# A decoder block in float32: seven products in another order, feature groups 4, 6, 6, 6, and a compressed attention branch stacked to 128 rows

## The chip, the cores and the metric

The kernel runs on one core of a Trainium2 chip. The metric is the device time of one execution in microseconds (us); each figure for a kernel is the median of several executions. The five engines of the core are called by the short names of the profile: PE (TensorE: matrix products and transposes), PEld (its weight loads), DVE (VectorE), ACT (ScalarE), POOL (GpSimd) and SP (SyncE, which issues most transfers). Each engine works through a list of its own in a fixed order.

## The reference

One block on a sequence of 512 tokens with 1024 features, batch 1, all in float32:

```python
h = rmsnorm(x, norm_mix_w); z = h @ w_in          # split into u, v | q, k_c, v_c, k_s, v_s, k_w, v_w, gates
a = gmlp_group(u, v, ...)                         # spatial gating inside chunks of 128 tokens
kc, vc = compress(k_c, ...), compress(v_c, ...)   # 31 compressed positions for each of 2 key/value heads
o = g0 * attention(q, kc, vc) + g1 * selected(q, k_s, v_s) + g2 * window(q, k_w, v_w)   # 8 heads of 64
x = x + concat(rmsnorm(a), rmsnorm(o)) @ w_o
h = rmsnorm(x, norm_ffn_w)
x = x + (silu(h @ w_gate) * (h @ w_up)) @ w_down  # 2816 hidden features
return rmsnorm(x, final_norm_w)
```

## The kernel before, in words

**Precision.** A float32 operand is held as two parts, a high one (`..h`, a copy on ACT by `copy_a`) and a low one (`..l`, the rest, made on DVE by `sub`). A product of two such operands is three matmuls (`mm3`): high by high, high by low, low by high. Tokens come in four tiles of 128.

**Attention.** For each token tile i and each key/value head kv (four query heads hang on one), `score` makes the scores `s`, DVE takes a minimum, ACT the exponential, POOL scales with the gate (`scale_p`). Then the tile is worked off in units: `turn` transposes four heads of probabilities on PE (`ptp`), splits them into high and low (`PT`: an ACT copy and a DVE subtraction of 512 columns), and `apply` multiplies them with the values `Vt` into one bank `o`. The last unit of each (i, kv) is the compressed branch: `cmp_probs` leaves probabilities `sc` over 32 positions for each head, `turn` transposes 128x32 pieces, and `apply` makes two matmuls with `VC`, whose inputs have 32 rows. After kv = 1, `out_norm` transposes the tile's result (`pto`) for its norm. The output projection `project` (banks `po`: eight for its part 0, then eight for part 1, each of 12 matmuls) stands in PE's list between these steps where the scheduler finds room.

**Feed-forward.** 22 blocks f of 128 hidden features; `gate_up(f)` makes 48 matmuls into `gu`. After the blocks of one group, `down` multiplies by `w_down` in the way of Strassen and Winograd: halves of the tokens and of the output columns, and instead of eight products seven (M1 to M7), each for two token tiles c = 0, 1 and all pairs of blocks in the group, three matmuls each. Banks A, B and C (two each) hold them; a bank is read by DVE in `accumulate`, which adds 128x512 to the stream `x2` (in the rows: x<-pA and the like), and some products go on in the same bank. Their weights come from the raw `wd_r` through differences on DVE (`diffs`, `t2_of`, `t4_of`), an ACT copy and a DVE subtraction, into `wh`, a ring of eight buffers that the gate and up weights share.

**End.** For each token tile the final norm: two squares over half a row on ACT (`rstd_halves`), the power on POOL, a multiplication by the norm's weights on DVE, a scale on ACT for one half and one DVE instruction for the other, and two transfers out.

**What sets the order.** The tile framework's scheduler writes each engine's list from the code's order, the dependencies and the buffers. PE's list is therefore not the code's order, and a change in one place moves instructions in others.

The lines that the prediction speaks of: `score` L543, `turn` L611, `apply` L626, `project` by the helper lines L114 to L116, `accumulate` L748, the two splitting helpers L79 (ACT) and L76 (DVE), the end L827 to L832.

Of the kernel before, what the change touches and what calls it, by code (L numbers as in the profile page):

```python
# [8 lines left out]
F32 = mybir.dt.float32  # L9
F32R = mybir.dt.float32r  # L10
# [8 lines left out]
P = 128  # L19
# [13 lines left out]
FFN_GROUPS = (6, 6, 6, 4)  # L33
# [8 lines left out]
def hybrid_gmlp_nsa_kernel(  # L42
# [282 lines left out]
    VC = cp.tile([32, NKV, P], F32R, name="VC")  # L325
# [20 lines left out]
    def compress_end(nm):  # L346
# [22 lines left out]
        else:  # L369
# [5 lines left out]
            copy_a(VC[:NCMP, :, 0:HD], vc)  # L375
            sub(VC[:NCMP, :, HD:P], vc, VC[:NCMP, :, 0:HD])
# [196 lines left out]
    def cmp_probs(i):  # L573
# [18 lines left out]
        for kv in range(NKV):  # L592
            PC[i, kv] = s[:, kv * 4:kv * 4 + 4]
# [8 lines left out]
    PTs, outs, oraws, rstd_b = {}, {}, {}, [None] * NT  # L602

    def turn(u):
        gi, j, br = UNITS[u]
        i, kv, b0 = GROUPS[gi]
        rows = P if j is not None else 32
        pt = bank("T", [P, 4, P], f"ptp{u}")
        for hh in range(4):
            src = probs[gi][:, hh, br, j * P:(j + 1) * P] if j is not None else PC[i, kv][:, hh]  # L610
            nc.tensor.transpose(pt[:rows, hh], src, ident)  # L611
        ptf = pt.rearrange("p h c -> p (h c)")[:rows]
        PTs[u] = t4([P, 2, S], F32R, f"PT{u}")
        copy_a(PTs[u][:rows, 0], ptf)
        sub(PTs[u][:rows, 1], ptf, PTs[u][:rows, 0])

    def apply(u):
# [3 lines left out]
        rows, v = (32, VC[:, kv]) if last else (P, Vt[:, b0 + br, j, kv])  # L621
# [129 lines left out]

    def down(gi, pairs):
# [5 lines left out]
        banks = {}  # L758
# [29 lines left out]

        product("M1", 0, "A", True, lambda r: r[:, 0, 0])
        for c in range(2):  # L790
            accumulate(2 + c, 0, banks["A", c])
        product("M5", 3, "C", True, lambda r: r[:, 0, 0], diffs)
        for c in range(2):
            accumulate(c, 1, banks["C", c])
        product("M6", 4, "A", False, lambda r: r[:, 0, 0], t2_of)
        for c in range(2):
            accumulate(2 + c, 1, banks["A", c])
        product("M2", 2, "B", True, lambda r: r[:, 1, 0])
        for c in range(2):
# [23 lines left out]
    for t in (2, 3, 0, 1):  # L823
        y = b8([P, DM], F32, f"y{t}")
        r = rstd_halves(x2[t], y, f"y{t}")
        rows = slice(t * P, (t + 1) * P)
        nc.vector.tensor_tensor(out=y[:, 0:512], in0=x2[t][:, 0:512], in1=onw[:, 0:512], op=OP.mult)  # L827
        nc.scalar.activation(y[:, 0:512], y[:, 0:512], AF.Copy, scale=r)
        nc.scalar.dma_start(out[rows, 0:512], y[:, 0:512])
        nc.vector.scalar_tensor_tensor(out=y[:, 512:], in0=x2[t][:, 512:], scalar=r, in1=onw[:, 512:],  # L830
                                       op0=OP.mult, op1=OP.mult)
        nc.sync.dma_start(out[rows, 512:], y[:, 512:])  # L832
# [31 lines left out]
```

## Time and profile before

| | |
|---|---|
| median of 3 runs | 631.84 us (631.25 to 632.08) |
| the profiled execution | 630.91 us, its span 629.2 us |
| PE busy | 606.5 us, 96% of the span |
| DVE busy | 411.3 us, 65% |
| ACT busy | 298.7 us, 47% |
| attention, first compressed scores to the last `o` matmul | 141.0 to 252.3 us |
| feed-forward on PE | 276.5 to 617.8 us |
| after PE's last matmul | 617.8 to 629.2 us |

The span runs from the first to the last instruction of the profiled execution; 1.7 us of its time lie outside. A busy PE is not PE at its peak: matmuls are pipelined, their durations overlap, and what one costs is read from the distance between the starts of two that follow each other.

### The profile page before, as it was taken

To read this page: it belongs to the slowest core of one execution; us is meant where nothing else is said; L and a number is where in the kernel's file an instruction comes from. 1 tells how busy PE (TensorE), PEld (TensorE's weight loads), DVE (VectorE), ACT (ScalarE), POOL (GpSimd) and SP (SyncE) were. 2 spreads that over 40 slices of the span, in tenths; PEclk is the share of its full clock that TensorE was granted. 3 is DMA by queue.
4 is the path that set the end of the run, shared out by engine and by line. 5 is a ranking of instruction groups with operands and counts; after the bars stand their busy time and mean duration, and the time that the engine had idled before them with its cause. 6 is when DMAs were issued, how large, how long until landed. Compare 5 with 4: busy or idle time off the path is not lost.

```text
span 629.2 us, 7754 instructions
## 1 busy us (share of the span) xinstructions
PE 606.5 (96%) x2847; PEld 489.9 (78%) x2847; DVE 411.3 (65%) x735; ACT 298.7 (47%) x544; POOL 68.1 (11%) x113
## 2 busy tenths in 40 slices
PE   7999899999999989999999999999999999999992
PEld 6778778787777667798887888887888888888871
DVE  4752778557887986746377944387844387844596
ACT  5753367467866784444234423234423235423244
POOL 3100100015434570100000000000000000000001
PEclk8999999999999999999999999999999999999997
DMA  8452535541000200059510383310373310350003
GB/s 316 147 140 63 171 107 167 161 172 64 1 2 0 76 26 1 2 162 300 157 51 0 121 247 95 95 45 1 126 242 100 95 41 1 131 170 0 2 0 133
DMA packets 73637, 61.85 MB, mean 98 GB/s; under 512 B 3696, under 2 KB 64128, under 8 KB 73600
## 3 DMA queue, kind: packets, MB, share of 16 engines
q1 hardware_dynamic: 73024, 60.32, 30.8%
q10 hardware_dynamic: 576, 1.05, 0.4%
q8 instruction: 22, 0.36, 0.2%
q14 instruction: 15, 0.12, 0.1%
HBM read 59.27 MB, written 2.10 MB: 98 GB/s over the span
## 4 chain that ended last, share of the span: by engine, by line
PE 87%; DVE 5%; DMA 2%; ACT 2%; POOL 1%; issue 1%; SPq 0%; POOLq 0%; ACTq 0%; DVEq 0%
PE gu L115 13%; PE gu L116 13%; PE gu L114 13%; PE o L626 4%; PE pA L114 3%; PE ptp L611 3%; PE pA L115 3%; PE pA L116 3%; PE s L543 2%; PE po L115 2%; PE po L116 2%; PE po L114 2%; PE pC L114 2%; PE pC L116 2%; PE pC L115 2%; PE z_v L116 1%
## 5 line engine op out<-in xcount | busy, mean ns | idle before, releaser
L115 PE MATMUL gu<-h2l,wg_h 128*128 128x512 f32 x168 | 65.4, 389 | 0.0
L114 PE MATMUL gu<-h2h,wg_h 128*128 128x512 f32 x168 | 65.4, 389 | 0.0
L116 PE MATMUL gu<-h2h,wu_l 128*128 128x512 f32 x168 | 65.4, 389 | 0.0
L115 PE MATMUL gu<-h2l,wu_h 128*128 128x512 f32 x168 | 65.4, 389 | 0.0
L116 PE MATMUL gu<-h2h,wg_l 128*128 128x512 f32 x168 | 65.4, 389 | 0.0
L114 PE MATMUL gu<-h2h,wu_h 128*128 128x512 f32 x168 | 65.4, 389 | 0.0
L79 ACT ACTIVATE wu_h<-wu_r 128x1024 fp32r<-128x1024 f32 x21 | 22.3, 1061 | 65.0 <-PE gu L115 48.5
L76 DVE TENSOR_TENSOR wg_l<-wg_r,wg_h 128x1024 fp32r<-128x1024 f32 x21 | 25.7, 1224 | 41.2 <-ACT wg_h L79 40.9
L675 DVE TENSOR_TENSOR sg<-gu,sg 128x512 f32<-128x512 f32 x22 | 15.2, 692 | 56.4 <-PE gu L116 56.4
L79 ACT ACTIVATE wg_h<-wg_r 128x1024 fp32r<-128x1024 f32 x21 | 22.3, 1060 | 45.7 <-PE gu L115 40.8
L167 POOL TENSOR_TENSOR rstd_y<-s_y,mhalf 128x1 f32<-128x1 f32 x4 | 3.0, 755 | 349.5 <-DVE s_y L164 347.0
L548 ACT ACTIVATE P<-P,nm 128x128 f32<-128x128 f32 (+3 forms) x64 | 35.5, 558 | 7.6 <-DVE nm L546 7.5
L114 PEld LDWEIGHTS gu<-h2h,wu_h 128*128 128x128 f32 x168 | 31.6, 188 | 6.6
L82 POOL TENSOR_SCALAR P<-P,sm 128x128 f32<-128x128 f32 (+3 forms) x64 | 33.6, 544 | 28.3 <-DVE sm L555 25.4
L116 PEld LDWEIGHTS gu<-h2h,wg_l 128*128 128x128 f32 x168 | 31.6, 188 | 6.5
L114 PEld LDWEIGHTS gu<-h2h,wg_h 128*128 128x128 f32 x168 | 31.5, 188 | 6.5
L115 PEld LDWEIGHTS gu<-h2l,wu_h 128*128 128x128 f32 x168 | 31.6, 188 | 6.5
L116 PEld LDWEIGHTS gu<-h2h,wu_l 128*128 128x128 f32 x168 | 31.5, 188 | 6.5
L115 PEld LDWEIGHTS gu<-h2l,wg_h 128*128 128x128 f32 x168 | 31.5, 188 | 6.5
L76 DVE TENSOR_TENSOR PT<-ptp,PT 128x512 fp32r<-128x512 f32 (+1 forms) x48 | 31.8, 681 | 6.3 <-ACT PT L79 5.9
L79 ACT ACTIVATE PT<-ptp 128x512 fp32r<-128x512 f32 (+1 forms) x48 | 27.0, 591 | 14.0 <-PE ptp L611 13.8
L546 DVE CUSTOM_DVE_ANT_0 P<-s,maskw 128x128 f32<-128x128 f32 (+3 forms) x64 | 29.4, 479 | 5.7 <-PE s L543 2.9
(502 smaller groups left out, 1522.9 us busy)
## 6 DMA issues: line engine op xcount, KB each, us to landing
wg_r<-in_w_gate_dram SPq DMA_DIRECT2D x22, 512.0 KB, 3.9
wu_r<-in_w_up_dram SPq DMA_DIRECT2D x22, 512.0 KB, 3.9
wd_r<-in_w_down_dram SPq DMA_DIRECT2D x11, 1024.0 KB, 8.5
wo_r<-in_w_o_dram SPq DMA_DIRECT2D x8, 512.0 KB, 4.3
x_sb<-in_x_dram SPq DMA_DIRECT2D x4, 512.0 KB, 8.8
wv_r<-in_w_in_dram SPq DMA_DIRECT2D x4, 512.0 KB, 7.5
wu_r<-in_w_in_dram SPq DMA_DIRECT2D x4, 512.0 KB, 3.8
w1k_r<-in_cmp_k_w_dram SPq DMA_DIRECT2D x4, 512.0 KB, 3.9
```

What stands on the lines that cost most here:

```text
L76: return (eng or nc.vector).tensor_tensor(out=o, in0=a, in1=hi.bitcast(F32), op=OP.subtract)
L79: return nc.scalar.activation(o, a, AF.Copy)
L82: nc.gpsimd.tensor_scalar(out=o, in0=a, scalar1=s, scalar2=1.0, op0=OP.mult, op1=OP.mult)
L114: nc.tensor.matmul(ps, lhsT=sh, rhs=mh, start=first, stop=False, skip_group_check=more)
L115: nc.tensor.matmul(ps, lhsT=sh, rhs=ml, start=False, stop=False, skip_group_check=more)
L116: nc.tensor.matmul(ps, lhsT=sl, rhs=mh, start=False, stop=last, skip_group_check=more)
L543: nc.tensor.matmul(sb, lhsT=q, rhs=KAB[kv][:, a, b0:b0 + nbr, :n], start=(a == 0), stop=(a == 1))
L546: nc.vector.tensor_tensor_reduce(out=pr, in0=sb[:, br], in1=maskw[:, S - n:], scale=-0.125, scalar=BIG, op0=OP.add, op1=OP.min, accum_out= ...
L548: e = nc.scalar.activation(pr, pr, AF.Exp, bias=nm[b], scale=-1.0, accum_out=sm[b])
L611: nc.tensor.transpose(pt[:rows, hh], src, ident)
L626: nc.tensor.matmul(o.rearrange("p h c -> p (h c)"), lhsT=v, rhs=PTs[u][:rows, a], start=(first and a == 0), stop=(last and a == 1))
L675: nc.vector.tensor_tensor(out=own, in0=pg[1], in1=own, op=OP.mult)
```

## The change

Three things are changed. (1) The compressed branch: `VC` becomes 128 rows high and holds each head's values four times over, in row ranges by head and by part, with zeros elsewhere; `cmp_probs` puts the high and the low part of the probabilities of both heads side by side (`pc`, 128 columns), `turn` transposes once for both kv, keeps only an ACT copy (`PTC`), and `apply` makes one matmul for each (i, kv). (2) `down`: the groups are 4, 6, 6, 6 blocks instead of 6, 6, 6, 4; the products come in the order M1, M2, M5, M6, M3, M7, M4 instead of M1, M5, M6, M2, M7, M3, M4; M2's banks B stay open over the groups and are added once, in the last. (3) The end: tiles 2 and 3 are finished ahead of the last addition to tiles 0 and 1, and these take their second half of columns first.

```diff
-FFN_GROUPS = (6, 6, 6, 4)
+FFN_GROUPS = (4, 6, 6, 6)
...
-    VC = cp.tile([32, NKV, P], F32R, name="VC")
+    VC = cp.tile([P, NKV, P], F32R, name="VC")
...
-            copy_a(VC[:NCMP, :, 0:HD], vc)
-            sub(VC[:NCMP, :, HD:P], vc, VC[:NCMP, :, 0:HD])
+
+            for h in range(NKV):
+                for a in range(2):
+                    r0 = h * HD + a * 32
+                    copy_a(VC[r0:r0 + NCMP, h, 0:HD], vc[:, h])
+                    sub(VC[r0:r0 + NCMP, h, HD:P], vc[:, h], VC[r0:r0 + NCMP, h, 0:HD])
...
-        for kv in range(NKV):
-            PC[i, kv] = s[:, kv * 4:kv * 4 + 4]
+
+        pc = t2([P, 4, NKV, 2, 32], F32R, f"pc{i}")
+        sv = s.rearrange("p (k h) n -> p h k n", k=NKV)
+        copy_a(pc[:, :, :, 0], sv)
+        sub(pc[:, :, :, 1], sv, pc[:, :, :, 0])
+        PC[i] = pc
...
-        rows = P if j is not None else 32
+        if j is None and kv > 0:
+            return
         pt = bank("T", [P, 4, P], f"ptp{u}")
         for hh in range(4):
-            src = probs[gi][:, hh, br, j * P:(j + 1) * P] if j is not None else PC[i, kv][:, hh]
-            nc.tensor.transpose(pt[:rows, hh], src, ident)
-        ptf = pt.rearrange("p h c -> p (h c)")[:rows]
+            src = (probs[gi][:, hh, br, j * P:(j + 1) * P] if j is not None
+                   else PC[i][:, hh].rearrange("p k a n -> p (k a n)").bitcast(F32))
+            nc.tensor.transpose(pt[:, hh], src, ident)
+        ptf = pt.rearrange("p h c -> p (h c)")
+        if j is None:
+            PTC[i] = t2([P, S], F32R, f"PTc{i}")
+            copy_a(PTC[i], ptf)
+            return
...
-        rows, v = (32, VC[:, kv]) if last else (P, Vt[:, b0 + br, j, kv])
...
-        for a in range(2):
-            nc.tensor.matmul(o.rearrange("p h c -> p (h c)"), lhsT=v, rhs=PTs[u][:rows, a],
-                             start=(first and a == 0), stop=(last and a == 1))
+        of = o.rearrange("p h c -> p (h c)")
         if not last:
+            for a in range(2):
+                nc.tensor.matmul(of, lhsT=Vt[:, b0 + br, j, kv], rhs=PTs[u][:, a],
+                                 start=(first and a == 0), stop=False)
             return
+        nc.tensor.matmul(of, lhsT=VC[:, kv], rhs=PTC[i], start=False, stop=True)
...
+        last_group = gi == len(FFN_GROUPS) - 1
+
+        def add(t0, hf, tag):
+            for c in range(2):
+                accumulate(t0 + c, hf, banks[tag, c])
+
         product("M1", 0, "A", True, lambda r: r[:, 0, 0])
...
+        add(2, 0, "A")
+
+        product("M2", 2, "B", gi == 0, lambda r: r[:, 1, 0])
+        if last_group:
+            add(2, 0, "B")
         product("M5", 3, "C", True, lambda r: r[:, 0, 0], diffs)
...
+        add(0, 1, "C")
         product("M6", 4, "A", False, lambda r: r[:, 0, 0], t2_of)
...
+        add(2, 1, "A")
+        product("M3", 6, "C", False, lambda r: r[:, 1, 1])
+        add(2, 1, "C")
         product("M7", 5, "A", False, lambda r: r[:, 0, 1])
...
+        add(0, 1, "A")
         product("M4", 1, "A", False, lambda r: r[:, 1, 0], t4_of)
...
+        if not last_group:
+            add(0, 0, "A")
...
-    for t in (2, 3, 0, 1):
+    def finish(t, order):
...
+    for t in (2, 3):
+        finish(t, (0, 1))
+    for t in range(2):
+        accumulate(t, 0, banks["A", t])
+    for t in range(2):
+        finish(t, (1, 0))
```

How the lists move is shown at three places. The first is PE's list in token tile 1, where the second head's compressed unit is worked off; before (`sc` are the probabilities of the compressed branch, `o` the result's bank, `s` scores of the tiles that follow, `ptp` transposes of other units):

```order
L611 MATMUL ptp_1647<-ident,sc_1363 32x128 x2
L645 MATMUL pto_1663<-ident,oraw_1556 128x128 x2
L543 MATMUL s_3_1753<-KAB_555,QS_558 128x384 x2
L543 MATMUL s_0_1812<-KAB_555,QS_558 128x384 x2
L114 MATMUL po_2334<-wo_s,mixah 128x512
L626 MATMUL o_1614<-PT_1652,VC 128x512
L115 MATMUL po_2334<-wo_s,mixah 128x512
L116 MATMUL po_2334<-wo_s,mixal 128x512
L543 MATMUL s_1_1817<-KAB_555,QS_558 128x384 x2
L114 MATMUL po_2334<-wo_s,mixah 128x512
L626 MATMUL o_1614<-PT_1652,VC 128x512
L611 MATMUL ptp_1704<-ident,P_1577 128x128 x4
```

and the same unit now:

```order
L115 MATMUL po_2280<-wo_s,mixah 128x512
L116 MATMUL po_2280<-wo_s,mixal 128x512
L114 MATMUL po_2294<-wo_s,mixah 128x512
L641 MATMUL o_1616<-PT_1634,Vt 128x512
L641 MATMUL o_1616<-PT_1644,Vt 128x512
L660 MATMUL pto_1656<-ident,oraw_1555 128x128
L641 MATMUL o_1616<-PT_1644,Vt 128x512
L644 MATMUL o_1616<-PTc_1552,VC 128x512
L660 MATMUL pto_1656<-ident,oraw_1555 128x128
L621 MATMUL ptp_1697<-ident,P_1579 128x128 x4
```

The four transposes of this head (two of them head the list of before) and one of its two `VC` matmuls are gone. The second place is PE's list around the last `o` matmul of the attention, before (`po_2432` is the third bank of the projection's part 1):

```order
L626 MATMUL o_2163<-PT_2241,VC 128x512
L645 MATMUL pto_2252<-ident,oraw_2121 128x128
L626 MATMUL o_2163<-PT_2241,VC 128x512
L645 MATMUL pto_2252<-ident,oraw_2121 128x128
L115 MATMUL po_2432<-wo_s,mixbh 128x512
L116 MATMUL po_2432<-wo_s,mixbl 128x512
L114 MATMUL po_2446<-wo_s,mixbh 128x512
```

and now (`po_2378` is the first bank of part 1):

```order
L115 MATMUL po_2378<-wo_s,mixbh 128x512
L641 MATMUL o_2146<-PT_2214,Vt 128x512
L644 MATMUL o_2146<-PTc_2101,VC 128x512
L116 MATMUL po_2378<-wo_s,mixbl 128x512
L114 MATMUL po_2392<-wo_s,mixbh 128x512
```

Before, 34 of the 96 matmuls of part 1 stood ahead of the last `o` matmul (two full banks and ten of the third); now 11 do, so 23 projection matmuls moved from inside the attention to behind it. The third place is DVE's list at the end, before (`x_1` holds token tiles 2 and 3, `x_0` tiles 0 and 1; `pA_4898` and `pA_4905` are the banks of the last product M4; `y` are the output tiles 2, 3, 0, 1 in this order):

```order
L748 TENSOR_TENSOR x_0_1171<-pA_4898,x_0_1171 128x512
L830 SCALAR_TENSOR_TENSOR y_5044<-x_1_1172,rstd_y_5049,onw 128x512
L748 TENSOR_TENSOR x_0_1171<-pA_4905,x_0_1171 128x512
L166 TENSOR_TENSOR s_y_5058<-s_y_5058 128x1
L827 TENSOR_TENSOR y_5057<-x_1_1172,onw 128x512
L830 SCALAR_TENSOR_TENSOR y_5057<-x_1_1172,rstd_y_5062,onw 128x512
L164 TENSOR_SCALAR s_y_5071<-s_y_5071 128x1
L827 TENSOR_TENSOR y_5070<-x_0_1171,onw 128x512
L166 TENSOR_TENSOR s_y_5071<-s_y_5071 128x1
L164 TENSOR_SCALAR s_y_5084<-s_y_5084 128x1
L827 TENSOR_TENSOR y_5083<-x_0_1171,onw 128x512
```

and now (`pA_4809` first for M7, then, two rows from the end of what is shown, for M4):

```order
L763 TENSOR_TENSOR x_0_1177<-pA_4809,x_0_1177 128x512
L849 SCALAR_TENSOR_TENSOR y_5004<-x_1_1178,rstd_y_5009,onw 128x512
L166 TENSOR_TENSOR s_y_5018<-s_y_5018 128x1
L164 TENSOR_SCALAR s_y_5033<-s_y_5033 128x1
L846 TENSOR_TENSOR y_5032<-x_0_1177,onw 128x512
L849 SCALAR_TENSOR_TENSOR y_5017<-x_1_1178,rstd_y_5022,onw 128x512
L763 TENSOR_TENSOR x_0_1177<-pA_4799,x_0_1177 128x512
L164 TENSOR_SCALAR s_y_5046<-s_y_5046 128x1
L846 TENSOR_TENSOR y_5045<-x_0_1177,onw 128x512
L763 TENSOR_TENSOR x_0_1177<-pA_4809,x_0_1177 128x512
L166 TENSOR_TENSOR s_y_5033<-s_y_5033 128x1
L849 SCALAR_TENSOR_TENSOR y_5032<-x_0_1177,rstd_y_5037,onw 128x512
```

All work of tiles 2 and 3 and the first halves of tiles 0 and 1 now stand ahead of the last addition out of PSUM.

## Rows read from the trace of the kernel before

**Rows 1.** The page: span and instructions, and each engine's busy time.

```profile
span 629.2 us, 7754 instructions
PE 606.5 (96%) x2847; PEld 489.9 (78%) x2847; DVE 411.3 (65%) x735; ACT 298.7 (47%) x544; POOL 68.1 (11%) x113
```

**Rows 2.** Stretches: length, then PE, PEld, DVE, ACT, POOL busy (instructions), clock, DMA.

```profile
141.00:252.30 111.30, 107.38 (x561) 80.34 (x560) 89.00 (x265) 79.93 (x209) 48.74 (x77) 1.00 0.08 26
276.50:617.80 341.30, 341.08 (x1518) 280.94 (x1518) 215.01 (x302) 126.11 (x176) 0.55 (x1) 1.00 0.32 99
617.80:629.20 11.40, 0.01 (x1) 0.00 (x0) 5.73 (x14) 4.83 (x10) 2.47 (x3) 0.66 0.49 184
...
220.00:240.00 20.00, 18.41 (x98) 13.70 (x97) 17.70 (x36) 15.34 (x33) 11.43 (x14) 1.00 0.08 24
```

**Rows 3.** The chain of waits in the attention, by engine and line.

```profile
by line: PE o L626 24.2%; PE ptp L611 18.1%; PE s L543 13.9%; PE po L115 8.1%; PE po L116 7.7%; PE po L114 7.6%; PE ptc L576 2.9%; DVE P L546 2.8%; POOL P L82 2.3%; ACT PT L79 2.2%; DVE sc L583 2.1%; DVE sm L555 1.7%; PE pto L645 1.6%; issu
```

**Rows 4.** Timeline of PE in the last group: start, duration, line, what.

```profile
616.06 0.39 PE L115 MATMUL pA<-wd9M,ah 128*128 128x512 f32 x1
616.29 0.39 PE L116 MATMUL pA<-wd9M,al 128*128 128x512 f32 x1
```

**Rows 5.** Timeline of PE around one matmul with 32 input rows.

```profile
177.91 0.40 PE L114 MATMUL po<-wo_s,mixah 128*128 128x512 f32 x1
178.24 0.50 PE L626 MATMUL o<-PT,VC 32*128 32x512 f32 x1
178.67 0.66 PE L611 MATMUL ptp<-ident,P 128*128 128x128 f32 x4
```

**Rows 6.** Matmuls that read VC (count, ns); then PE's timeline at transposes.

```profile
L626 PE MATMUL o<-PT,VC x16: 489/492/500, 154.9 to 251.0; 32*128 32x512 f32 x16
...
199.53 0.38 PE L611 MATMUL ptp<-ident,P 128*128 128x128 f32 x2
199.75 0.60 PE L611 MATMUL ptp<-ident,sc 128*32 128x128 f32 x4
```

**Rows 7.** Groups by shape on DVE and ACT (busy us, mean ns, idle).

```profile
L76 DVE TENSOR_TENSOR PT<-ptp,PT 32x512 fp32r<-32x512 f32 x8 | 5.4, 674 | 1.1 <-ACT PT L79 1.1
L683 DVE TENSOR_TENSOR ss<-sg 128x256 f32<-128x256 f32 x22 | 9.3, 422 | 0.4
...
L79 ACT ACTIVATE PT<-ptp 128x512 fp32r<-128x512 f32 x40 | 22.6, 593 | 12.0 <-PE ptp L611 11.7
L79 ACT ACTIVATE PT<-ptp 32x512 fp32r<-32x512 f32 x8 | 4.6, 580 | 2.0 <-PE ptp L611 2.0
L79 ACT ACTIVATE KC<-cps_k 64x62 fp32r<-64x62 f32 x4 | 0.9, 216 | 0.1
```

**Rows 8.** Timeline of DVE in the second group's products.

```profile
456.24 1.22 DVE L76 TENSOR_TENSOR wu_l<-wu_r,wu_h 128x1024 fp32r<-128x1024 f32 x1 [0.83 <-ACT wu_h L79]
457.39 0.68 DVE L748 TENSOR_TENSOR x<-pC,x 128x512 f32<-128x512 f32 x1
```

**Rows 9.** Timeline of the end; transfers out (KB, median us to landing).

```profile
617.42 0.39 PE L116 MATMUL pA<-wd10M,al 128*128 128x512 f32 x1
618.46 0.68 DVE L748 TENSOR_TENSOR x<-pA,x 128x512 f32<-128x512 f32 x1
619.18 0.63 ACT L162 ACTIVATE y<-x 128x512 f32<-128x512 f32 x1
621.82 0.99 POOL L167 TENSOR_TENSOR rstd_y<-s_y,mhalf 128x1 f32<-128x1 f32 x1 [1.60 <-DVE s_y L164]
623.51 0.15 DVE L166 TENSOR_TENSOR s_y<-s_y 128x1 f32<-128x1 f32 x1
624.33 0.75 DVE L830 SCALAR_TENSOR_TENSOR y<-x,rstd_y,onw 128x512 f32<-128x512 f32 x1 [0.66 <-POOL rstd_y L167]
625.08 0.37 ACTq L829 DMA_DIRECT2D out_dram<-y  x1
...
out_dram<-y ACTq DMA_DIRECT2D x4, 256.0 KB, 2.8
```

More of the change, by code (lines that the diff above doesn't have):

```diff
@@ L156, in square_sum, with rstd_halves @@
         return acc
-    def rstd_halves(src, junk, name):
+    def rstd_halves(src, junk, name, order=(0, 1)):
         ms = small([P, 2], f"s2_{name}", "s2")
-        for hf in range(2):
+        for n, hf in enumerate(order):
             c = slice(hf * 512, hf * 512 + 512)
-            nc.scalar.activation(junk[:, c], src[:, c], AF.Square, scale=DM ** -0.5, accum_out=ms[:, hf:hf + 1])
-            if hf == 0:
+            nc.scalar.activation(junk[:, c], src[:, c], AF.Square, scale=DM ** -0.5, accum_out=ms[:, n:n + 1])
+            if n == 0:
                 nc.vector.tensor_scalar(out=ms[:, 0:1], in0=ms[:, 0:1], scalar1=EPS, scalar2=None, op0=OP.add)
@@ L601, in hybrid_gmlp_nsa_kernel @@
             UNITS.append((gi, None, 0))
-    PTs, outs, oraws, rstd_b = {}, {}, {}, [None] * NT
+    PTs, PTC, outs, oraws, rstd_b = {}, {}, {}, {}, [None] * NT
     def turn(u):
@@ L606, in turn @@
         i, kv, b0 = GROUPS[gi]
-        rows = P if j is not None else 32
+        if j is None and kv > 0:
+            return
         pt = bank("T", [P, 4, P], f"ptp{u}")
         for hh in range(4):
-            src = probs[gi][:, hh, br, j * P:(j + 1) * P] if j is not None else PC[i, kv][:, hh]
-            nc.tensor.transpose(pt[:rows, hh], src, ident)
-        ptf = pt.rearrange("p h c -> p (h c)")[:rows]
+            src = (probs[gi][:, hh, br, j * P:(j + 1) * P] if j is not None
[6 more added lines that the diff above has]
+            return
         PTs[u] = t4([P, 2, S], F32R, f"PT{u}")
-        copy_a(PTs[u][:rows, 0], ptf)
-        sub(PTs[u][:rows, 1], ptf, PTs[u][:rows, 0])
+        copy_a(PTs[u][:, 0], ptf)
+        sub(PTs[u][:, 1], ptf, PTs[u][:, 0])
     def apply(u):
@@ L748, in accumulate @@
         nc.vector.tensor_tensor(out=x2[t][:, c], in0=src, in1=x2[t][:, c], op=OP.add)
+    banks = {}
     def down(gi, pairs):
@@ L757, in down @@
             raws.append(r)
-        banks = {}
         def product(name, slot, tag, first, src, before=None):
@@ L822, in hybrid_gmlp_nsa_kernel @@
         f0 += nb
-    for t in (2, 3, 0, 1):
+    def finish(t, order):
         y = b8([P, DM], F32, f"y{t}")
-        r = rstd_halves(x2[t], y, f"y{t}")
+        r = rstd_halves(x2[t], y, f"y{t}", order)
         rows = slice(t * P, (t + 1) * P)
[L827 to L830, printed above, removed]
-                                       op0=OP.mult, op1=OP.mult)
-        nc.sync.dma_start(out[rows, 512:], y[:, 512:])
+        c, d = (slice(hf * 512, hf * 512 + 512) for hf in order)
+        nc.vector.tensor_tensor(out=y[:, c], in0=x2[t][:, c], in1=onw[:, c], op=OP.mult)
+        nc.scalar.activation(y[:, c], y[:, c], AF.Copy, scale=r)
+        nc.scalar.dma_start(out[rows, c], y[:, c])
+        nc.vector.scalar_tensor_tensor(out=y[:, d], in0=x2[t][:, d], scalar=r, in1=onw[:, d],
+                                       op0=OP.mult, op1=OP.mult)
+        nc.sync.dma_start(out[rows, d], y[:, d])
+    for t in (2, 3):
[4 more added lines that the diff above has]
+        finish(t, (1, 0))
     fp.__exit__(None, None, None)
```

16 lines of the change are left out of this document (removed).

## The prediction

> **What bounds the kernel now.** The page comes first: PE is busy 96% of the span, DVE 65%, ACT 47% [rows 1], so the first question is always what PE does. The table by stretch then says where that average hides different limits [rows 2]. In the feed-forward (276.5 to 617.8 us) PE is busy 341.08 of 341.30 us and DVE 215.01: nothing but PE's own work counts there, and two matmuls of 512 columns that follow each other start 0.23 us apart [rows 4]. That distance is my price of a matmul; the 0.39 us that the row gives as a duration overlaps the next one. After PE's last matmul come 11.4 us in which PE does nothing [rows 2]: a pure chain of DVE, ACT, POOL and transfers. The attention (141.0 to 252.3 us) is mixed: PE busy 107.38 of 111.30 us, but DVE 89.00 and ACT 79.93 as well. The chain of waits decides who leads there: its pieces on PE add up to 24.2 + 18.1 + 13.9 + 8.1 + 7.7 + 7.6 + 2.9 + 1.6 = 84%, those on DVE, ACT and POOL to the rest [rows 3]. So PE leads in the attention, not alone.
>
> **The compressed branch.** Sixteen matmuls read `VC` [rows 6], two in each of the eight (i, kv). Each has 32 input rows, and PE's timeline around one shows what it costs in a stream: the matmul ahead of it starts 0.33 us earlier, the next instruction 0.43 us later [rows 5]. Two full-height matmuls would take 0.23 + 0.23 there, so the short one costs 0.30 more than a full one: some 0.53 us. The change makes eight of 128 rows instead: 16 x 0.53 - 8 x 0.23 = 6.6 us of PE less, if a full-height one pays no such gap, as the others in the stream do not. Of the 32 transposes of 128x32 pieces 16 remain, as 128x128. Two whole transposes take 199.53 to 199.75, 0.11 each [rows 6], and I price either shape at that: 16 x 0.11 = 1.8. PE loses 8.4 us of work.
>
> The Trainium skill has a rule against this (TensorE: Matmul & The Clock Gate, section Why this matters for your kernels): a single matmul with 32 input rows takes the same time as one with 128. By it the branch would give 8 x 0.23 + 1.8 = 3.6 us, not 8.4. [rows 5] speak against it for a matmul among full-height ones; the Trainium skill's TensorEngine Tiling (Array Packing), section Key Properties, has a change of tiling mode drain the engine, which would be such a gap on either side.
>
> DVE loses eight subtractions of 0.674 and gains four over 256 columns, at 0.422 by the nearest row [rows 7]: 5.4 - 1.7 = 3.7 us less. ACT loses eight copies of 0.580 and gains four of 0.593 and four of half the width [rows 7], which cannot be more: about even. The filling of `VC` costs ACT and DVE three more instructions each, at 0.216 or under [rows 7]; `VC` is first read at 154.9 us [rows 6], after the projections, so PE's matmuls there cover them (0.6 us if they did not). The extra copy and subtraction lengthen the way from probabilities to transposes by under 0.593 + 0.422; the transposes stand behind all other units of their group, which covers it. What queues behind that subtraction on DVE is the next `score`; four times 0.422 is its price, counted above.
>
> How much of 8.4 us reaches the end? Between nothing (the attention goes at the pace of DVE and ACT) and 8.4 + 3.7 = 12.1 (the waits for DVE shrink as well). PE's share of the chain, 84%, gives 7.0. But PE's list says that 23 projection matmuls, 23 x 0.23 = 5.2 us, have moved from inside the attention to behind it. They cost the same there, yet they no longer fill waits: DVE must get its attention work done in about 111.3 - 7.0 - 5.2 = 99.1 us. It has 89.0 - 3.7 for it, 86%. In the densest slice now DVE has 17.70 of 20 us, 88%, with PE still at 18.41 [rows 2], so this is possible but not free. I take 0.6 off: **6.4 us**.
>
> **The order in `down`.** The number of matmuls, 462, stays, and so does the number of groups. Six additions of M2's banks go from DVE, 0.68 each by the addition in [rows 8], from a stretch where DVE has 126 us to spare: worth nothing. The new order costs something at one place: M4 follows M7 in the same banks A with no product between, where M3 stood before. M4's first token tile may not write until DVE has added M7's. DVE's list now has there: M3's second addition, the split of the next gate weights, M7's first addition, the split of the next up weights, M7's second addition. Before, an addition rode behind such a split without harm: the split began at 456.24, after 0.83 idle for ACT, and the addition at 457.39 [rows 8]. Now PE waits behind it. From M7's end: the up weights' buffers are free about then, the ACT copy takes some 1.1 (an estimate from the split's 1.22), the split 1.22, the addition 0.68, overlapping a little, so it ends near 2.3; M4's first token tile has 9 x 0.23 = 2.1 us of work before its second needs that bank. About 0.2 late, in two groups (the scheduler put gate matmuls ahead of M4 in the first, and the last has no next weights): I take a **loss of 0.3 us**, between nothing and 3 x (1.22 + 0.68) = 5.7. On SP's list the load for the fourth pair of blocks waits for a buffer that the first group's M4 frees, and the up weights of block 5 stand behind it; PE wants those only after 72 more matmuls, 16 us, which covers a load and a split.
>
> **The end.** Now the last transfer is issued at 625.08, 7.3 us after PE's last matmul ends (617.42 + 0.39) [rows 9]; four tiles are finished one after the other there. In the new list tiles 2 and 3 close with M3, and M7 and M4 (36 x 0.23 = 8.3 us) lie over their finish; of tiles 0 and 1 the first halves are squared early. What is left behind PE: the addition to the start of the square 0.72 (618.46 to 619.18), the square 0.63, reading out its sum some 0.2 (an estimate from the 0.15 of the small sum's own row), DVE's multiplication for tile 0, 0.75, which stands ahead of tile 1's small sum, from that sum to the multiplication for tile 1 between 0.82 (623.51 to 624.33) and 1.3 (with a power of 0.99 on POOL, as at 621.82, behind a sum of 0.15), this multiplication 0.75, and ACT's second issue 0.37 [rows 9]: 4.2 to 4.7 us, and I take 4.7. That is 2.6 less. A transfer lands 2.8 us after its issue [rows 9]; the four last now leave within about 2.5 us and share the engines, for which I take off 0.3: **2.3 us**. The bounds are 1.4 (two transfers wait for half a landing) and 3.1 (4.2 and no loss in the transfers).
>
> **The sum.** 6.4 - 0.3 + 2.3 = 8.4 us less. Against the profiled execution, 630.91, that is 622.5; the median, 631.84, lies 0.9 above it, so 623.4.
>
> **The rivals.** (a) The gap around short matmuls is not theirs, but a wait that their places have (for `PT`, or the bank), and stays with the full-height ones: 3.6 x 0.84 = 3.0 instead of 6.4, and 626.8. For it: each stands where a unit ends. Against it: the gap behind the matmul in [rows 5] is on PE, with no wait noted. (b) M4 waits for M7's addition at the full price of 5.7 in three groups: 628.8. For it: the split stands ahead of the addition in DVE's list; against it, that split has been early enough to finish before. (c) On the other side: DVE and ACT set the pace of the attention, its end stays at 252.3, and the 23 matmuls then run behind it: +5.2 + 0.3 - 2.3, slower by 3.2, 635.0. It decides as soon as the stretch up to the last `o` matmul shrinks by less than 3.2 us. For it: 16% of the chain and the 88% slice; against it, DVE loses work too. (d) The waits shrink with DVE's 3.7 us: 12.1 instead of 6.4, 617.7. (e) Losses and gains cancel: 631.8.
>
> **Chances.** Forecast 0.62 (its own range 620.5 to 626.0), (a) 0.12, (b) 0.08, (c) 0.06, (d) 0.08, (e) 0.04. A measurement of this kernel can tell some 0.2%, 1.3 us, from no change. Faster: 0.62 + 0.12 + 0.08 + 0.08 = 0.90; same 0.04; slower 0.06. The range 619.0 to 629.5 takes in (a) and (b) and leaves out (c), (e) and the far side of (d).
>
> **What the profile of the changed kernel would show.** Eight `VC` matmuls of 128*128, the next start 0.23 us after each; if it is 0.4, (a) holds. The last `o` matmul 9 to 14 us before 252.3, and PE's first full `gu` matmul some 6 earlier than now; if `o` comes less than 3.2 earlier, (c). Between M7 and M4 less than 0.5 us of idle PE in a group; more, (b). From PE's last matmul to the last transfer issued 4.3 to 5.2 us, not 7.3. The prediction is wrong if the attention's waits grow by what PE saved.

## The result, and the profile after

| | before | after |
|---|---|---|
| median of 4 runs each, on one chip | 631.96 us | 622.69 us (621.91 to 623.46) |
| ratio, 95% interval | | 0.9854 [0.9837, 0.9872] |
| the profiled execution, its span | 630.91, 629.2 us | 623.25, 621.5 us |

The change makes the kernel 9.3 us faster by the medians, 7.7 us by the two profiled executions; 8.4 was predicted. Three cuts through the profiled executions say where the 7.7 us came from: the stretch from the first compressed scores (`st`, which start at 137.5 and 137.6 us) to the first `gu` matmul of 512 columns, from there to PE's last matmul, and what comes after it.

| stretch | before | after | gained | predicted |
|---|---|---|---|---|
| first `st` to first full `gu` | 145.28 | 141.30 | 4.0 | 6.4 |
| first full `gu` to the end of PE's last matmul | 335.00 | 334.77 | 0.2 | -0.3 |
| after PE's last matmul | 11.4 | 7.8 | 3.6 | 2.3 |

The sum was nearly right because its errors ran against each other: the attention gave less than forecast, the end more. That far its closeness is luck.

The page of the kernel after, with the granted clock in 40 slices; the first two of these lines answer to [rows 1]:

```profile
span 621.5 us, 7683 instructions
...
PE 597.8 (96%) x2823; PEld 489.5 (79%) x2823; DVE 401.7 (65%) x728; ACT 297.4 (48%) x547; POOL 68.5 (11%) x113
...
PEclk9999999999999997999999999999999999999998
```

PE lost 8.7 us of busy time in all. One slice is new: the sixteenth digit, from 233 to 249 us, is a 7 where PE had its full clock before ([rows 2] have 1.00 for the whole stretch). The stretches of the kernel after, with the columns of [rows 2] (length, busy time of PE, PEld, DVE, ACT and POOL, granted clock, DMA):

```profile
141.00:244.50 103.50, 96.26 (x516) 77.00 (x515) 82.69 (x258) 77.37 (x205) 49.06 (x77) 0.97 0.09 29
276.50:613.70 337.20, 337.20 (x1492) 277.77 (x1490) 211.82 (x301) 127.14 (x179) 1.92 (x2) 1.00 0.32 99
613.70:621.50 7.80, 0.01 (x1) 0.00 (x0) 2.83 (x6) 2.82 (x6) 1.10 (x2) 0.70 0.53 202
```

In the feed-forward PE is busy for all of its 337.20 us: M4 right behind M7 waits for nothing. In the attention, on the other hand, PE is idle for 7.2 of 103.5 us, where [rows 2] have 3.9 of 111.3. PE's waits in that stretch, longest sum first, name the place:

```profile
PE o L641 <- ACT PT L79: 4.6, 1, 4.6
PE ptp L621 <- POOL P L82: 2.3, 5, 0.7
```

One wait of 4.6 us is new. The timelines of ACT, SP and POOL (q marks an engine's sequencer that issues a transfer; in brackets the idle time ahead and what ended it) show what stands behind it:

```profile
225.97 0.59 ACT L79 ACTIVATE PT<-ptp 128x512 fp32r<-128x512 f32 x1
227.58 1.34 ACT L79 ACTIVATE PT<-ptp 128x512 fp32r<-128x512 f32 x2 [1.03 <-PE ptp L621]
234.24 1.06 ACT L79 ACTIVATE wg_s<-wg_r 128x1024 fp32r<-128x1024 f32 x1 [5.32 <-DMA wg_r<-in_w_gate_dram]
235.20 1.06 ACT L79 ACTIVATE PT<-ptp 128x512 fp32r<-128x512 f32 x2
...
219.94 0.37 SPq L87 DMA_DIRECT2D wo_r<-in_w_o_dram  x1
230.28 0.37 SPq L87 DMA_DIRECT2D wg_r<-in_w_gate_dram  x1
...
227.87 4.70 POOL L76 TENSOR_TENSOR wo_s<-wo_r,wo_s 128x1024 fp32r<-128x1024 f32 x2
```

Read them from the bottom. POOL subtracts the low part of two blocks of output weights (`wo_s`) from 227.87, 2.35 us each. The raw weights share three buffers, so SP can issue the load of the first gate weights `wg_r` only when the first of these is done, at 230.28. It lands 3.9 us later. ACT's list has the copy of these weights, which PE needs only some 30 us later, ahead of two `PT` copies; ACT waits 5.32 us for the load, the `PT` copies behind it wait too, and PE waits for those.

In the kernel before the same load and the same copy stand here:

```profile
211.77 0.37 SPq L87 DMA_DIRECT2D wg_r<-in_w_gate_dram  x1
...
233.98 1.05 ACT L79 ACTIVATE wg_s<-wg_r 128x1024 fp32r<-128x1024 f32 x1
```

There the load leaves 74.2 us after the first `st`, long before its copy, which waits for nothing; now it leaves 92.6 us after it, 18.4 later. The buffer is freed by the second block of part 1's output weights, and the splitting of those weights has moved: ACT's first copy of them starts 61.1 us after the first `st` before and 76.1 now, POOL's subtraction of the second block 71.8 and 90.2. PE's timeline after the wait:

```profile
235.83 0.79 PE L641 MATMUL o<-PT,Vt 128*128 128x512 f32 x1 [4.60 <-ACT PT L79]
236.42 0.63 PE L114 MATMUL po<-wo_s,mixbh 128*128 128x512 f32 x1
236.85 0.63 PE L115 MATMUL po<-wo_s,mixbh 128*128 128x512 f32 x1
...
241.72 0.40 PE L114 MATMUL po<-wo_s,mixbh 128*128 128x512 f32 x1
241.96 0.40 PE L115 MATMUL po<-wo_s,mixbh 128*128 128x512 f32 x1
```

Matmuls of 512 columns start 0.43 us apart there instead of 0.23, up to 241.5; the granted clock of 235.83 to 241.50 is 0.51, the lower of the two levels (1.2 GHz). Ten such matmuls at 0.20 more are 2.0 us; six transposes lie among them, and with those and the `o` matmul behind them the same 17 instructions take 5.9 us here and 3.6 in a kernel without the wait (`gate_behind` below, from 232.06 to 235.65). So by this count the new wait costs 4.6 + 2.3 = 6.9 us, and that the attention is 4.0 us shorter all the same means that some 10.9 us were gained there.

What was gained is seen at a matmul that reads `VC`, now of 128 rows; it answers to [rows 5]:

```profile
155.87 0.40 PE L114 MATMUL po<-wo_s,mixah 128*128 128x512 f32 x1
156.10 0.40 PE L644 MATMUL o<-PTc,VC 128*128 128x512 f32 x1
156.34 0.60 PE L621 MATMUL ptp<-ident,P 128*128 128x128 f32 x4
```

It starts 0.23 us after the one ahead, and the next starts 0.24 later: the gaps of 0.33 and 0.43 are gone. The end of the kernel after, beside [rows 9]:

```profile
613.32 0.39 PE L116 MATMUL pA<-wd10M,al 128*128 128x512 f32 x1
614.20 0.68 DVE L763 TENSOR_TENSOR x<-pA,x 128x512 f32<-128x512 f32 x1
614.92 0.63 ACT L162 ACTIVATE y<-x 128x512 f32<-128x512 f32 x1 [0.54 <-DVE x L763]
616.52 0.55 POOL L167 TENSOR_TENSOR rstd_y<-s_y,mhalf 128x1 f32<-128x1 f32 x1 [0.94 <-DVE s_y L166]
617.10 0.75 DVE L849 SCALAR_TENSOR_TENSOR y<-x,rstd_y,onw 128x512 f32<-128x512 f32 x1 [0.66 <-POOL rstd_y L167]
```

The multiplication ends at 617.85, 4.1 us after PE, and the last transfer is issued 4.2 us after PE, where it was 7.3 before.

### The profile page after: what moved, and what is told of

It reads as the page before. It is cut to its first block, busy times and chain, and to the rows that moved or that the text cites. A ratio compares the mean times of both kernels' runs of the same rounds, so it can differ in the third digit from the quotient of the medians.

```text
span 621.5 us, 7683 instructions
## 1 busy us (share of the span) xinstructions
PE 597.8 (96%) x2823; PEld 489.5 (79%) x2823; DVE 401.7 (65%) x728; ACT 297.4 (48%) x547; POOL 68.5 (11%) x113
## 4 chain that ended last, share of the span: by engine, by line
PE 84%; DVE 4%; DMA 3%; ACT 3%; POOL 3%; issue 2%; SPq 0%; POOLq 0%; ACTq 0%; DVEq 0%
PE gu L115 13%; PE gu L116 13%; PE gu L114 13%; PE o L641 3%; PE pA L114 3%; PE pA L116 3%; PE pA L115 3%; PE s L547 3%; PE ptp L621 3%; PE po L115 2%; PE po L116 2%; PE po L114 2%; PE pC L116 1%; PE pC L115 1%; PE pC L114 1%
## 5 line engine op out<-in xcount | busy, mean ns | idle before, releaser
L641 PE MATMUL o<-PT,Vt 128*128 128x512 f32 x80 | 32.0, 451 | 4.8 <-ACT PT L79 4.6
L76 DVE TENSOR_TENSOR wu_l<-wu_r,wu_h 128x1024 fp32r<-128x1024 f32 x21 | 25.6, 1219 | 4.9 <-ACT wu_h L79 4.9
```

The costliest lines, as they stand in the source:

```text
L76: return (eng or nc.vector).tensor_tensor(out=o, in0=a, in1=hi.bitcast(F32), op=OP.subtract)
L641: nc.tensor.matmul(of, lhsT=Vt[:, b0 + br, j, kv], rhs=PTs[u][:, a], start=(first and a == 0), stop=False)
```

## The experiments

Two theories stood at the start. One: the parts add up, the stacked branch gains some 11 us of which the wait for the gate weights takes back 6.9. Its rival: ACT, DVE and POOL set the pace at the end of the attention anyway, and the wait is only where this shows, so taking it away would move it. Each ratio below is against the kernel before on the same chip; kernels of one group ran on one chip.

**First group: the parts, the wait, the height of the matmul.**

`stack_only`: the kernel before with the change's edits to `VC`, `cmp_probs`, `turn` and `apply`.

> The kernel before with the compressed branch stacked, and nothing else of the change. Theory (the parts add up, and this part also brings the new wait): the last `o` matmul comes near 243 us and the first full `gu` matmul near 279, both as in the whole change, PE waits some 4.6 us near 231 for a PT copy that stands behind the copy of gate weights, and the time is 3.9 us under the kernel before, near 628.0. Rival (the wait comes from the parts together): no such wait, and 9 to 10 us less, near 622.5.

627.79 us, 0.9923 [0.9902, 0.9945], 4.3 us less. `st` to the first full `gu` takes 141.40 us, like the 141.30 of the whole change, and the wait is there alone:

```profile
PE o L641 <- ACT PT L79: 4.6, 1, 4.6
```

`down_end_only`: the kernel before with the groups, products, open bank and end of the change.

> The kernel before with the groups, the order of the products, the open bank and the end of the change, and the compressed branch as it was. Theory (the parts add up): the attention and the first full `gu` matmul stay at 252.3 and 282.8 us, the feed-forward takes about 341.1 us, PE's end to the last transfer issue 4.2 us; 3.8 us under the kernel before, near 628.1. Rival (the whole change's end is only fast because the attention's order differs): less than 3 us.

628.25 us, 0.9931 [0.9912, 0.9951], 3.8 us less; PE's end at 617.43, the rest 8.0 us. Together the parts give 4.3 + 3.8 = 8.1 us, the whole change 9.3, the same within their intervals. The wait belongs to the stacked branch and not to what stands behind it in the program.

`gate_behind`: the changed kernel, with the splits of the first gate and up weights (for each an ACT copy and a DVE subtraction) ordered behind the last `PT` copy.

```diff
-        copy_a(PTs[u][:, 0], ptf)
+        last_pt[0] = copy_a(PTs[u][:, 0], ptf)
...
-            ws = [load_cols(w, 0, KD, f * P, P, f"w{'gu'[a]}{f}", spare=f == 0, behind=last_norm if f == 1 else None,
+            ws = [load_cols(w, 0, KD, f * P, P, f"w{'gu'[a]}{f}", spare=f == 0, behind=last_norm if f == 1 else last_pt[0] if f == 0 else None,
```

> The changed kernel with the split of the block-0 gate and up weights ordered behind the last PT copy on ACT; nothing is left out. Theory (the copy of gate weights that waits for its transfer holds up the PT copies behind it): the 4.6 us wait near 231 is gone, PE keeps its granted clock there, the last `o` matmul comes some 6 us earlier, near 237, and the time is 5 to 6.5 us under the changed kernel, 616 to 618. Rival (ACT, DVE and POOL set the pace of the attention's end anyway, the wait comes back at another place): within 1.5 us of the changed kernel, 621 to 623.

617.74 us, 0.9764 [0.9747, 0.9781]. Its SP and ACT at that place, and two of its stretches (the first from the first `st` to the first full `gu`):

```profile
231.03 0.37 SPq L87 DMA_DIRECT2D wg_r<-in_w_gate_dram  x1
...
234.43 0.60 ACT L79 ACTIVATE PT<-ptp 128x512 fp32r<-128x512 f32 x1 [0.98 <-PE ptp L622]
234.92 1.05 ACT L79 ACTIVATE wg_s<-wg_r 128x1024 fp32r<-128x1024 f32 x1
...
139.00:273.84 134.84, 130.95 (x741) 107.35 (x740) 101.91 (x295) 94.28 (x241) 51.89 (x82) 1.00 0.16 50
224.00:236.00 12.00, 11.97 (x64) 9.08 (x64) 6.87 (x11) 8.00 (x12) 11.15 (x9) 1.00 0.26 78
```

The load is issued as late as in the changed kernel, and nobody waits for it: the copy stands behind the last `PT` copy, which itself waits for PE. PE is busy 11.97 of the 12 us where it had waited, at the full clock, with POOL at 93%. The stretch is 134.84 us, 6.5 less than the changed kernel's and 10.4 less than before. The rival, that the wait would come back elsewhere, falls. The stretch of the kernel before, in the same columns, tells work from waits:

```profile
137.51:282.79 145.28, 139.97 (x765) 108.83 (x764) 109.12 (x299) 96.01 (x241) 51.46 (x82) 1.00 0.15 46
```

PE's busy time is 9.0 us less in `gate_behind` and its idle time 1.4 less (5.3 and 3.9).

`gate_behind_short`: the same instructions in the same places, eight of them of 32 rows.

```diff
-        nc.tensor.matmul(of, lhsT=VC[:, kv], rhs=PTC[i], start=False, stop=True)
+        r = slice(kv * HD, kv * HD + 32)
+        nc.tensor.matmul(of, lhsT=VC[r, kv], rhs=PTC[i][r], start=False, stop=True)
```

> The kernel gate_behind whose eight matmuls of the compressed branch read only 32 of the 128 input rows (the low part of the compressed probabilities is left out). The same number of instructions in the same places. Theory (a short matmul among full-height ones costs a gap on either side): the next start after each is near 0.43 us and the one ahead 0.33, 0.3 more for each, 8 x 0.3 = 2.4 us more PE time, and the time is 1.5 to 2.4 us over gate_behind. Rival (the gap belongs to the places): no gap and no difference.

619.66 us, 0.9797 [0.9778, 0.9817], 1.9 us over `gate_behind`. PE's timeline at the first of them, first in `gate_behind_short`, then in `gate_behind`:

```profile
157.20 0.40 PE L114 MATMUL po<-wo_s,mixah 128*128 128x512 f32 x1
157.53 0.50 PE L646 MATMUL o<-PTc,VC 32*128 32x512 f32 x1
157.95 0.55 PE L622 MATMUL ptp<-ident,P 128*128 128x128 f32 x3
```

```profile
156.64 0.40 PE L114 MATMUL po<-wo_s,mixah 128*128 128x512 f32 x1
156.87 0.39 PE L645 MATMUL o<-PTc,VC 128*128 128x512 f32 x1
157.10 0.60 PE L622 MATMUL ptp<-ident,P 128*128 128x128 f32 x4
```

0.33 and 0.42 in the one, 0.23 and 0.23 in the other, at the same place. Over all eight the starts ahead and behind add up to 6.28 us against 4.02: 2.3 us for eight short matmuls, 0.28 each. The gap is the short matmul's own. The 1.9 us of the time are not as clean a measure. In the profiled execution of `gate_behind_short` PE ran at the lower clock for 3.4 us, some 1.7 us of loss that `gate_behind` does not have; before it PE had waited 0.53 us twice for POOL's scaling:

```profile
149.67:153.09 3.42, 3.42 (x11) 2.84 (x10) 1.26 (x8) 2.32 (x9) 1.28 (x2) 0.51 0.00 0
```

Its first `st`, on the other hand, came 1.4 us earlier (last section). The price is therefore taken from the starts. The Trainium skill (TensorE: Matmul & The Clock Gate, section Why this matters for your kernels) says that a single matmul with 32 input rows takes the time of one with 128; by that this kernel would have lost nothing, and in this stream the measurement decides against it. That a change of the tiling mode drains the engine, as the Trainium skill has it (TensorEngine Tiling (Array Packing), section Key Properties), agrees with a gap on both sides; that this is the gap's reason, no run here shows.

**Second group: what the end is made of.** All four start from `gate_behind`.

`closed`: M2's banks are opened and added in each group.

```diff
-        product("M2", 2, "B", gi == 0, lambda r: r[:, 1, 0])
-        if last_group:
-            add(2, 0, "B")
+        product("M2", 2, "B", True, lambda r: r[:, 1, 0])
+        add(2, 0, "B")
```

> The kernel gate_behind with M2's banks closed and added to the stream in each group, as before the change: six additions of 0.68 us more on DVE, nothing left out. Theory (the feed-forward is PE's alone, DVE has over 100 us to spare there): the feed-forward's length changes by under 0.3 us, the time stays at 617.7, within 0.6. Rival (the additions queue ahead of something PE waits for, each at its full 0.68): 4.1 us more, 621.8.

619.47 us, 0.9803 [0.9787, 0.9818]. In the trace the full `gu` to PE's end takes 334.68 us against 334.61 in `gate_behind`, so the time contradicts the trace; it was measured again below.

`groups_old`: `FFN_GROUPS = (6, 6, 6, 4)`.

> The kernel gate_behind with the groups 6, 6, 6, 4 of before; nothing is left out. Theory (the group order matters only through what lies over the finish of tiles 2 and 3): M7 and M4 of the last group are 24 matmuls, 5.5 us, where 36, 8.3 us, stand in gate_behind, and the finish of those tiles takes DVE until some 7.6 us after M3, so PE's end to the last transfer issue grows from 4.15 to about 6.4 us; 1 to 2.5 us more, 618.7 to 620.2. Rival (the order of the groups is without effect): 617.7.

620.94 us, 0.9816 [0.9801, 0.983]. Its last stretch, then the last matmul of M3 (pC) and of M4 (pA), and the last multiplication on DVE:

```profile
610.73:620.53 9.80, 0.00 (x0) 0.00 (x0) 4.91 (x11) 3.50 (x7) 2.09 (x3) 0.68 0.57 214
...
604.90 0.39 PE L116 MATMUL pC<-wd10M,al 128*128 128x512 f32 x1
...
610.34 0.39 PE L116 MATMUL pA<-wd10M,al 128*128 128x512 f32 x1
...
616.06 0.75 DVE L850 SCALAR_TENSOR_TENSOR y<-x,rstd_y,onw 128x512 f32<-128x512 f32 x1 [0.66 <-POOL rstd_y L167]
```

From M3's last matmul to M4's are 5.4 us. DVE has eleven instructions left behind PE where the changed kernel has six, 4.91 us against 2.83, and the last multiplication ends 6.1 us after PE instead of 4.1. What comes after PE is 9.80 us against 7.83: the order of the groups is worth 2.0 us at the end, by what lies over the finish of tiles 2 and 3. The time is 3.2 us over `gate_behind`, more than the 1 to 2.5 expected; the profiled executions, 4.2 us apart, also differ by a first `st` 1.3 us later and a stretch from it to the first full `gu` 1.1 us longer, and neither was traced to the groups.

`end_old`: the last additions go back ahead of the finish of tiles 2 and 3, and all tiles take their first half first.

```diff
-        if not last_group:
-            add(0, 0, "A")
+        add(0, 0, "A")
...
-    for t in (2, 3):
-        finish(t, (0, 1))
-    for t in range(2):
-        accumulate(t, 0, banks["A", t])
-    for t in range(2):
-        finish(t, (1, 0))
+    for t in (2, 3, 0, 1):
+        finish(t, (0, 1))
```

> The kernel gate_behind with the code of the end as before the change (the last additions to tiles 0 and 1 ahead of the finish of tiles 2 and 3, first half of the columns first for all), with the new order of the products; nothing is left out. Theory (the early half squares and the early multiplication by the weights of tiles 0 and 1 are worth something by themselves): a square of 0.63 and two multiplications of 0.69 come back behind PE's end; PE's end to the last issue 5.4 to 6.2 us instead of 4.15, 1.2 to 2 us more, 618.9 to 619.7. Rival (the end is fast because M3 comes two products earlier, the code of the end does nothing): 617.7.

618.12 us, 0.9779 [0.9766, 0.9792], and 8.2 us after PE against 7.8: the theory fell, the code of the end is worth 0.3 us up to the last issue (4.5 us after PE against 4.2) and some 0.4 in all. The reason is in ACT's timeline of `end_old`:

```profile
607.73 0.63 ACT L162 ACTIVATE y<-x 128x512 f32<-128x512 f32 x1 [0.66 <-DVE x L764]
...
608.36 0.61 ACT L162 ACTIVATE y<-x 128x512 f32<-128x512 f32 x1
...
608.98 0.63 ACT L162 ACTIVATE y<-x 128x512 f32<-128x512 f32 x1
```

The scheduler had already put the half of tile 1 that is complete (608.36) ahead of the one that waits for the last addition (608.98), though the code names them the other way round.

`tail`: on DVE the last addition to tile 0 ahead of tile 3's last multiplication, the sum of tile 0 ahead of the last addition to tile 1, and on ACT the second square of tile 1 ahead of tile 0's scale (`second_half` is the square, the sum and the power of a tile, `leave` its scale, multiplication and transfers).

```diff
+    done = accumulate(0, 0, banks["A", 0])
+    after(done, SUM[3])
+    leave(3, dve=done)
+    second_half(0)
+    done = accumulate(1, 0, banks["A", 1])
+    after(done, SUM[0])
+    q = second_half(1)
+    leave(0, q, SUM[1])
+    leave(1)
```

> The kernel gate_behind with another order at the end: on DVE the last addition to tile 0 ahead of tile 3's last multiplication and that to tile 1 ahead of tile 0's, and on ACT the second square of tile 1 ahead of tile 0's scale; nothing is left out. Theory (after PE's end DVE's fixed order delays the chain square, power, multiplication of tile 1): the addition to tile 1 starts with PE's end instead of 0.5 us later, the small sum no longer stands behind a multiplication of 0.75; the last issue comes 0.8 to 1.2 us earlier after PE's end, 3.0 to 3.4 us, and the time is 616.5 to 617.0. Rival (the transfers, now closer together, share the engines and land as late as before): 617.7.

619.46 us, 0.9796 [0.9783, 0.981]; after PE come 8.4 us, not 7.8, and the last issue is no earlier, 4.3 us after PE. DVE's timeline shows why the issue did not move:

```profile
608.72 0.16 DVE L858 TENSOR_TENSOR s_y<-s_y 128x1 f32<-128x1 f32 x1
608.79 0.68 DVE L764 TENSOR_TENSOR x<-pA,x 128x512 f32<-128x512 f32 x1
610.26 0.16 DVE L858 TENSOR_TENSOR s_y<-s_y 128x1 f32<-128x1 f32 x1 [0.79 <-ACT y L856]
```

PE was done at 608.01, and the last addition stood behind tile 3's multiplication (to 608.58) and tile 0's small sum, which needs a square of ACT, until 608.79: 0.8 us after PE instead of 0.5. Tile 1's small sum then came without a multiplication ahead of it, as intended, but that multiplication now ran on DVE from 610.34 to 611.08 beside the last power on POOL, which took 0.99 us from 610.50 instead of 0.55 (last section). From the last issue to the end were 4.1 us besides, against 3.7; that is no answer to the rival, since kernels with one and the same end differ as much: 3.65 us in the changed kernel and 4.11 in `wo_dve`, 4.11 in the kernel before and 3.69 in `stack_only`.

**Third group: repeats on one chip, and who holds the buffer.**

> The changed kernel once more, as the baseline of the three others on the same chip: 621.5 to 624.

624.21 us, 0.9872 [0.9853, 0.989], with the same wait of 4.6 us.

> The kernel gate_behind once more, on the chip of the changed kernel: 4 to 6.5 us under it. If the gain of the first time was of the chip, less.

617.89 us, 0.9784 [0.9766, 0.9802], 6.3 us under the changed kernel on the same chip (the first time 617.74, 5.0 under its first median). The gain is the kernel's.

> The kernel closed once more, on the chip of gate_behind. In the traces the stretch on PE from the first full `gu` matmul to the last matmul was 334.68 us against 334.61, yet the medians, from two chips, lay 1.7 us apart. Theory (the six additions are hidden): within 0.6 us of gate_behind on the same chip. Rival (they cost): 1.2 us or more over it.

618.5 us, 0.9798 [0.9777, 0.982], 0.6 over `gate_again` with intervals that overlap, and 334.72 us against 334.71 in the trace. The six additions are hidden; no cost of them can be measured. Where the 1.7 us of the first comparison came from is not shown: the two profiled executions were only 0.7 us apart.

`wo_dve`: the changed kernel with the other engine for the subtractions of part 1's four output weights.

```diff
-                us.append(split(raw, [2, 512], f"wo{part}{hf}{g}", (nc.vector, nc.gpsimd)[part]))
+                us.append(split(raw, [2, 512], f"wo{part}{hf}{g}", nc.vector))
```

> The changed kernel with the low parts of the four output weights of part 1 subtracted on DVE instead of POOL; nothing is left out. Theory (the load of the gate weights waits for a raw buffer that POOL's subtraction of 2.4 us, behind other POOL work, holds): DVE makes it in 1.2 us right behind the ACT copy, the load is issued near 226.5 instead of 230.3 and lands near 230.4; the scheduler puts the copy of gate weights four PT copies earlier, so ACT still waits for it, 2 to 3 us instead of 5.3; PE's wait falls from 4.6 to under 2.5 us, and the time is 1.5 to 4 us under the changed kernel. Rival (the load is late because of SP's order or the transfer itself): issue stays near 230.3, and with the copy earlier in ACT's list PE's wait grows to 6 to 7 us, 2 to 4 us slower than the changed kernel.

620.23 us, 0.9815 [0.9792, 0.9837], 4.0 us under the changed kernel on the same chip. SP, then ACT, then PE's wait:

```profile
228.85 0.37 SPq L87 DMA_DIRECT2D wg_r<-in_w_gate_dram  x1
...
232.90 1.06 ACT L79 ACTIVATE wg_s<-wg_r 128x1024 fp32r<-128x1024 f32 x1 [1.79 <-DMA wg_r<-in_w_gate_dram]
...
PE o L641 <- ACT PT L79: 0.2, 1, 0.2
```

Counted from the first `st` (140.18 here, 139.67 in `after_again`, whose load is issued at 232.26), the load leaves 3.9 us earlier, ACT waits 1.8 us instead of 5.3 and PE 0.2 instead of 4.6. The stretch is 136.89 us against 140.76 in `after_again` and 135.41 in `gate_again`, although PE ran 3.5 us of it (from 152.4) at a granted clock of 0.54. So the buffer under POOL's subtraction made the load late by 3.9 us, and the copy's place in ACT's list made the lateness cost time: two edits that share nothing else each remove the wait. The greater part of the 18.4 us by which the load comes later than before is the later place of part 1's weights in the lists; no run puts them back.

The best version is `gate_behind`: 617.7 to 617.9 us.

## Why the prediction was right, and where its terms were off

**The compressed branch: the mechanism right, the loss mis-sized.** The price of a short matmul in a stream, some 0.30 over a full one, was measured at 0.28, and rival (a), that the gap stays at its places, is refuted at the places themselves (0.23 behind each of the eight) and by `gate_behind_short`. The branch is worth 10.4 us of the stretch when nothing else gets in the way (9.9 in `gate_again`), between the 8.4 of PE's work and the 12.1 with DVE's waits: 9.0 of it are work of PE and 1.4 are waits, where (d) had 3.7 for waits. The step that failed is "I take 0.6 off" for a denser DVE: DVE was not what became late. The loss was one transfer. The prediction saw that 23 projection matmuls moved to behind the attention and priced their work; it did not follow their weights. Those were split later as well, their buffers came free later, the load of the gate weights left 18.4 us later, and a copy that needed it stood ahead of copies that PE needed. By the count above that took 6.9 us; taking the wait away gave 6.5 us of the stretch back the first time and 5.4 on one chip (140.76 and 135.41). So the net was 4.0 instead of 6.4, and the first full `gu` came 3.9 us earlier and not 6. The last `o` matmul starts at 243.1. The 252.3 that the prediction measures from is not its start before: that is 251.0, by [rows 6] (nor do the first compressed scores start at 141.0, but at 137.5). So it came 7.9 us earlier, less than the 9 to 14 forecast, and more than the 3.2 below which (c) would have decided. Of the signs listed, the last one ("the attention's waits grow by what PE saved") came true in part: PE's idle time grew by 3.3 us, 5.6 with the loss at the lower clock, where 8.4 were to be saved. Rival (c) had the shape of this, others late where PE is fast, but not its place.

**`down`: a loss that was not there.** For M4 right behind M7 0.3 us was taken; the stretch is 0.2 shorter, PE has no wait in it, and (b) falls. The addition behind the split of the up weights was in time. The six additions saved were costed at nothing, and `closed_again` agrees.

**The end: 3.6 instead of 2.3.** The forecast for PE's end to the last issue was 4.2 to 4.7 with 4.7 taken, and 4.2 was measured, 3.1 less than before: the power on POOL took 0.55 and not the 0.99 that made the upper bound. Transfers were to cost 0.3 more for sharing; from the last issue to the end of the span are 3.7 us against 4.1 before. That half microsecond is not the change's, though: it differs as much between kernels with the same end (see `tail`), so a cost of sharing was neither seen nor excluded, and the end is worth 3.1 us rather than 3.6. What brought it was in part another edit than the prediction put first: taken back alone, the order of the groups costs 2.0 us and the code of the end 0.3; the rest, that M3 comes ahead of M7, was not tried alone.

**The sum.** 4.0 + 0.2 + 3.6 - 0.1 (the attention began that much later) = 7.7 on the profile, against 6.4 - 0.3 + 2.3 = 8.4. The 622.7 us lie inside the range through errors of both signs; without the wait the time is 617.7, where (d) had put it, by 10.4 us in the stretch instead of (d)'s 12.1 and by the larger gain at the end.

## What to carry to other kernels

When PE gets faster in a stretch, list what must arrive from memory in that stretch, whose work frees the buffer that it is loaded into, and where its first user stands in each engine's list. Here work that moved behind the attention took its buffers along; a copy of weights that are needed 30 us later, placed ahead of copies that PE needs now, turned the late load into a loss, and an ordering edge gave 5 to 6 us back. In this stream a matmul of 32 rows cost 0.28 us more than one of 128, so pad or stack such a matmul. For a chain at the end of a program, ask what work of PE still lies over it: the size of the last group was worth 2.0 us, the order of the code 0.3 to 0.4.

## What the runs showed that was not expected

One wait of 4.6 us was followed by 5.7 us at the lower level of PE's clock (granted 0.51), which added 2.3 us to it; in the kernels without the wait the same work ran at 1.00. In two of those, `gate_behind_short` and `wo_dve`, PE ran some 3.5 us at the lower level at another place, near 150 us, after waits of at most 0.73 us for POOL; `gate_behind` has such waits there too and no fall.

The power on POOL at the end (`rstd_y`) has two lengths. In the 14 traces it runs 56 times: 0.92 to 1.00 us each time that it starts while DVE multiplies 512 columns by the norm's weights, 0.54 to 0.55 each time that it does not, an addition out of PSUM on DVE included. The 0.99 in [rows 9] is one of the first kind, the last power is of the second kind in every kernel but `tail`; the reason was not tested.

The opening, which no kernel here changes, is not equally long. The first 50 us on PE, of `closed_again` and then of `wo_dve` (start and end, length, PE busy and so on, granted clock):

```profile
9.60:60.00 50.40, 48.61 (x220) 38.57 (x221) 28.17 (x46) 28.93 (x51) 3.85 (x7) 1.00 0.47 141
```

```profile
9.60:60.00 50.40, 48.58 (x207) 38.83 (x208) 26.02 (x44) 26.91 (x49) 3.84 (x7) 0.93 0.46 138
```

At a granted clock of 0.93 PE got through 207 matmuls there, at 1.00 through 220, and the first `st` came at 140.2 and 137.5 us. Over all the traces it came between 137.5 and 140.3, which is about as much as the times of one kernel scatter and more than the 1.7 us that had seemed to be `closed`'s. What lowers the clock there in some executions stayed open; differences of a microsecond were therefore read from stretches that begin at the first `st`.
